# Prompt attention scores as plain float32 products in the two row halves of the array

## The chip, the cores and the metric

One Trainium2 chip, of which the kernel uses one NeuronCore. The core has five engines that run side by side: TensorE (matrix products, with a weight load ahead of each, in the profile PE and PEld), VectorE (DVE), ScalarE (ACT), GpSimd (POOL) and SyncE (SP), which here issues all DMAs. The metric is the device time of one execution in microseconds, less is better; what is given is the median of three runs.

## The reference

The kernel computes one step of a trunk of two layers for 512 prompt tokens and 32 sample tokens (8 sequences of 4 tokens), all in float32, with a model width of 1024. In each layer a normed input is projected, part of the projection goes to a retention group of 4 heads, part to an attention group of 8 heads of 64 columns; both outputs go through one output projection; then comes a feed-forward with a short convolution. Of the attention over the prompt, with which the change deals, the reference says:

```python
for window, dil in DIL_PATTERNS:
    ...
    s = jnp.einsum('brnqhd,brnkhd->brnhqk', qs, kb) * hd ** -0.5
    ...
    s = jnp.where(valid[None, None, :, None], s, -jnp.inf)
    m = jnp.max(s, axis=-1, keepdims=True)
    p = jnp.exp(s - m)
    den = jnp.sum(p, axis=-1, keepdims=True)
    o = jnp.einsum('brnqhk,brnkhd->brnqhd', p / den, vb)
    ...
return combine_by_denominator(outs, lses)
```

The kernel folds the three patterns into one softmax over all earlier keys: a bias that holds the logarithm of how many patterns see a key is added to the scores.

## The kernel before

All activations lie transposed, columns of the model on the 128 partitions and the 544 tokens along the free axis, as two chunks of 272. The big products (projection, output projection, feed-forward) are the main stream: 256 blocks of 128 output columns, and for each block and each 128 rows of weights three products of split parts. [...] ScalarE makes the high part of the weights (`split_w`, line 311), VectorE subtracts to get the low part (`wl` in the profile). The weights come in by DMA six half blocks ahead and are split three half blocks ahead.

Everything else is put between the steps of the main stream while the program is traced. Each job is a generator that yields what its next piece needs. A planner, class `Clock`, estimates from fixed costs when each engine reaches and ends every instruction; class `Stream` lets a piece go (`_ready`, line 180) when its operands should be there by that estimate: a piece of TensorE 0.30 us after them (`MARGIN`, line 145), a piece of another engine 0.25 us before them at the earliest (`SLACK`). The order of instructions on each engine is thus fixed before the kernel runs, and an engine that comes to an instruction whose operands are late waits there, with everything behind it.

Each layer begins with 28 projection blocks. For each pair of heads (`hp`, four pairs) there is a block of values, one of keys and one of queries; VectorE turns keys and queries by the rotary tables (`ra` once and `rb` four times a block, `rotary_out`, line 486), GpSimd adds the two terms into the tiles `ka` and `qa` (lines 494 and 495). The two heads of a pair lie in partitions 0 to 63 and 64 to 127 of the same tile. `att_pair` (line 544) then does a pair: it transposes the values, splits queries and keys, and runs `att_unit` (line 578) for four groups of 128 queries; unit i sees (i + 1) x 128 keys. `pairs` (line 919) runs pairs 0 and 2 in one generator and pairs 1 and 3 in another.

The split of a pair, for each of its two heads: ScalarE copies the head's queries to float32r (`qq`, 64 partitions) and its keys twice (`kk`, into both halves), VectorE subtracts to get the low part of the queries (into the other half of `qq`) and of the keys (`kl`). The scores of a unit are four products in float32r: for each head [q hi; q lo] x [k hi; k hi], over all 128 rows of the array, then for each head q hi x k lo, over its 64 rows; the second adds to the first in PSUM.

After the scores, for each head of a unit: VectorE adds the bias and takes the row maximum (`p<-sec,cst`), ScalarE takes the exponential with its sum, VectorE takes the reciprocal and scales `p`, TensorE transposes `p` (`sec<-cst,p`), ScalarE copies that out (`pt`), and TensorE multiplies by the values (`sec<-pt,vt`, the two heads in the array's column halves).

All tensor instructions go through one helper, so nearly all rows of the profile have line 112; operations are told apart by their tiles (`sec` is a PSUM tile of this side work, `ps` one of the main stream). Plain float32 products and products of the split parts both read as f32 there.

Of the kernel before, what the change touches and what calls it, by code (L numbers as in the profile page):

```python
# [9 lines left out]
F32 = mybir.dt.float32  # L10
F32R = mybir.dt.float32r
AF = mybir.ActivationFunctionType
OP = mybir.AluOpType
PSUM = bass.MemoryType.PSUM

DEPTH, D, SEQ, NB, T = 2, 1024, 512, 8, 4
# [41 lines left out]


class Clock:  # L60
    """Estimates when each engine reaches and ends the instructions that were traced, so that
    independent work is traced where its operands are likely to be there."""

    def __init__(self):
        self.now = dict.fromkeys(SEM, 0.0)
# [26 lines left out]


class Engine:
    """Hands instructions on to an engine of the core and to the clock."""

    def __init__(self, clock, kind, eng):
        self.clock, self.kind, self.eng = clock, kind, eng
# [16 lines left out]
    def charge(self, method, outs, ins, args, kw):  # L115
        c, kind = self.clock, self.kind
        n = free_size(outs[0]) if outs else 0
        if method == "dma_start":
            c.now["sp"] = max(c.now["sp"], c.when("sp", ins)) + 0.06
            c.dma = max(c.dma, c.now["sp"] + 0.8) + n * outs[0].shape[0] * 4 / 3.6e5  # L120
            c.wrote[c.key(outs[0])] = ("sp", c.dma + 1.0)
            return
        if kind == "pe":
            rows = outs[0].shape[0]
            if method == "transpose":
                cost = max(n, 128) * 2 / 2400
            elif (kw["lhsT"]).dtype == F32R:
                cost = max(n / 2400, 0.107)
            else:
                cost = max(n * 4 / 2400, 0.21) / (1 if rows > 64 else 128 // rows)  # L130
            cost += 0.003
        elif kind == "act":
            ptr = sum(free_size(i) == 1 for i in ins[1:])
            cost = 1.3 if method.startswith("preload") else n / 1200 + 0.093 * (1 + ptr)
        elif kind == "dve":
            half = method in ("tensor_scalar", "tensor_copy")
            cost = (n * (0.5 if half else 1) + 66 + (60 if len(ins) > 2 else 0)) / 960
        else:
            cost = 0.1 + n * (2.2 if len(ins) > 1 else 1.0) / 1000
        c.issue(kind, outs, ins, cost)  # L140
# [9 lines left out]


class Stream:
    """Places pieces of independent work between the steps of the main product stream. A generator
    yields what its next piece needs: its kind (the tensor engine, another engine, or a condition),
    its operands and its banks of PSUM."""

    def __init__(self, clock, share):
        self.clock = clock
# [66 lines left out]
def trunk(ctx: ExitStack, tc: tile.TileContext, xin, w_in, w_out, w_up, w_down, kc, vc, s0, sctx_d, params_d,  # L225
          consts_d, rope_d, y_o, kv_o, pret_o, sret_o, conv_o):
    nc = tc.nc
    clock = Clock()
    pe, act, dve, pool, sp = (Engine(clock, k, e) for k, e in (
        ("pe", nc.tensor), ("act", nc.scalar), ("dve", nc.vector), ("pool", nc.gpsimd), ("sp", nc.sync)))  # L230
# [3 lines left out]
    work = ctx.enter_context(tc.tile_pool(name="work", bufs=1))  # L234
# [10 lines left out]
    def blk(shape, dt=F32, s="b"):  # L245
        return work.tile(shape, dt, name=name(s), tag="blk", bufs=NBLK)

    def PE(*aps, banks=0):
        return need("pe", *aps, banks=banks)

    def EW(eng, *aps):
        return need(eng, *aps)
# [36 lines left out]
    def small(shape, s, bufs):  # L289
        return work.tile(shape, F32, name=name(s), tag=s, bufs=bufs)  # L290

# [1 line left out]
    main = []  # L293
    halves = []

# [7 lines left out]
    raw, split = {}, {}  # L303
# [29 lines left out]
        st.until(lambda: s in split)  # L333
        return split[s]

# [1 line left out]
    x = [cpool.tile([128, 2, HC], F32, name=f"x{n}") for n in range(KB)]  # L337
    par = cpool.tile([128, NPAR], F32, name="par")
    taps = cpool.tile([128, NCONV], F32, name="taps")
# [1 line left out]
    eps = cpool.tile([128, 1], F32, name="eps")  # L341
# [7 lines left out]
        st.until(lambda: len(evacs) < 2)  # L349
        return rotate(psum.tile([128, 2, 512], F32, name=name("ps"), tag="main", bufs=2), "main", 2)  # L350

# [1 line left out]
    class Norm:  # L353
        def __init__(self, idx):
            self.idx = idx
# [43 lines left out]
            return self.parts[k]  # L399

        def rsqrt(self, ps, shape):
            """Yields its steps; returns 1 / sqrt(mean + eps), with a Newton step on the table's value."""
            r, v, t = (blk(shape, F32, s) for s in ("rstd", "var", "tmp"))
            yield EW("act", *ps)
            for c, p in enumerate(ps):
                act.activation(r[:, c], p[:, :HC], AF.Ln, bias=eps, scale=1.0 / D)
            act.activation(r, r, AF.Exp, scale=-0.5)
            for c, p in enumerate(ps):
                dve.tensor_scalar(v[:, c], p[:, :HC], -0.5 / D, -0.5 * EPS, op0=OP.mult, op1=OP.add)
            done(len(ps))  # L410
            yield EW("dve", r)
            dve.tensor_mul(t, r, r)
            yield EW("dve", t)
            dve.tensor_mul(t, t, v)
            yield EW("dve", t)
            dve.scalar_tensor_tensor(r, t, 1.5, r, op0=OP.add, op1=OP.mult)
            return r
# [8 lines left out]
            self.rstd = yield from self.rsqrt(ps, [128, 2, HC])  # L426

    class Last(Norm):
        """Takes the last product stream by halves of the tokens."""

        def take(self, n, c, ps):
            if n == 0:
# [42 lines left out]
    def rhs_of(norm):  # L475
        return norm.part

# [1 line left out]
    def two(ap, w):  # L479
        return ap.rearrange("p (c n) -> p c n", c=2)  # L480

# [40 lines left out]
            st.spawn(gen(ps), "evac")  # L522
        return start

# [1 line left out]
    class Layer:  # L526
        pass

# [11 lines left out]
        for t in L.tab[first]:  # L540
            pool.tensor_mul(t, t, norm.rstd)

    # prompt attention of one pair of heads
    def att_pair(L, l, hp):
        q, k, v = L.qa[hp], L.ka[hp], L.va[hp]
        yield PE(v, banks=2)
        ps = sec([128, 4, 128])
        for c in range(4):
            pe.transpose(ps[:, c, :], v[:, c * 128:(c + 1) * 128], ident)
        ps2 = sec([32, 128])  # L550
        pe.transpose(ps2, v[:, SEQ:NT], ident)
        L.va[hp] = None
        yield EW("act", ps)
        vt = blk([128, 4, 128], F32, "vt")
        act.activation(vt, ps, AF.Copy)
        act.activation(L.vs[:, hp * 128:(hp + 1) * 128], ps2, AF.Copy)
        done(2)
        # float32 products as f32r parts: [q hi; q lo] x [k hi; k hi], then q hi x k lo
        qs, ks = [], []
        kl = blk([128, SEQ], F32R, "kl")  # L560
        for s in range(2):
            r, o = slice(64 * s, 64 * s + 64), slice(64 - 64 * s, 128 - 64 * s)
            kk, qq = blk([128, SEQ], F32R, "kk"), blk([128, SEQ], F32R, "qq")
            yield EW("act", q, k)
            act.activation(qq[r], q[r, :SEQ], AF.Copy)
            act.activation(kk[r], k[r, :SEQ], AF.Copy)
            act.activation(kk[o], k[r, :SEQ], AF.Copy)
            yield EW("dve", qq, kk)
            dve.tensor_sub(qq[o], q[r, :SEQ], qq[r].bitcast(F32))
            dve.tensor_sub(kl[r], k[r, :SEQ], kk[r].bitcast(F32))  # L570
            qs.append(qq)
            ks.append(kk)
        del q, k
        L.qa[hp] = L.ka[hp] = None
        for i in range(4):
            yield from att_unit(L, hp, i, qs, ks, kl, vt)

    def att_unit(L, hp, i, qs, ks, kl, vt):
        n = (i + 1) * 128
        ps, pr, ms, pts = [], [], [], []  # L580
        yield PE(*qs, *ks, kl, banks=2)
        for s in range(2):
            r = slice(64 * s, 64 * s + 64)
            t = sec([128, 512])
            pe.matmul(t[:, :n], lhsT=qs[s][:, i * 128:(i + 1) * 128], rhs=ks[s][:, 0:n], start=True, stop=False)
            ps.append(t)
        for s in range(2):
            r = slice(64 * s, 64 * s + 64)
            pe.matmul(ps[s][:, :n], lhsT=qs[s][r, i * 128:(i + 1) * 128], rhs=kl[r, 0:n], start=False, stop=True)
        for s in range(2):  # L590
            yield EW("dve", ps[s])
            p = blk([128, 512], F32, "p")
# [14 lines left out]
        for s in range(2):  # L607
            yield PE(pr[s], banks=1)
            t = sec([128, 4, 128])
# [9 lines left out]
        for j in range(i + 1):  # L619
            for s in range(2):  # L620
                pe.matmul(po[64 * s:64 * s + 64, :], lhsT=vt[:, j, 64 * s:64 * s + 64], rhs=pts[s][:, j, :],
                          start=j == 0, stop=j == i)
# [6 lines left out]
        L.steps += 1  # L629
        return IF(lambda: st.block >= at)  # L630

    # sample attention of four sequences; rows are (sequence, head, token)
    def att_sample(L, l, g):
        rows = [slice(32 * i, 32 * i + 32) for i in range(4)]
        for hp in range(4):
# [100 lines left out]
        L.cath[k] = (h, lo)  # L736
        L.cat[k] = None

    # retention of one head
    def ret_head(L, l, h):  # L740
        q, k, v = L.qr[h], L.kr[h], L.vr[h]
        qd = blk([128, 4, 128], F32, "qd")
# [6 lines left out]
        ps = sec([128, 4, 128])  # L749
# [7 lines left out]
        ps = sec([128, 4, 128])  # L757
# [7 lines left out]
        ps = sec([128, 4, 128])  # L765
# [4 lines left out]
        sm = blk([128, 4, 128], F32, "sm")  # L770
        dve.tensor_mul(sm, ps, C["dmask"][:, None, h * 128:(h + 1) * 128].to_broadcast([128, 4, 128]))
        done()
        # sample parts of this head
        yield PE(k, v, q, banks=1)
        ps = sec([32, 4, 128])
        pe.transpose(ps[:, 0, :], k[:, SEQ:NT], ident)
# [118 lines left out]
                store(sret_o[l, h, :, g * 4:g * 4 + 4, :], s)  # L895
        L.s0 = None

# [1 line left out]
    def mixer(l):  # L899
        L = Layer()  # L900
        norm = norms[l][0]
# [174 lines left out]
        for n in range(KB):  # L1076
            add_block(w_out[l, n, :, 0:4, :], 4, lambda k: L.cath[k], add_ret(n), pre=pre_ret if n == 0 else None)

# [1 line left out]
    def ffn(l):  # L1080
        norm, nxt = norms[l][1], norms[l + 1][0]
        F = Layer()
# [94 lines left out]
        mixer(l)  # L1177
        ffn(l)

# [1 line left out]
    first = norms[0][0]  # L1181
    act.preload_act_table_set("natural_log_exp_and_others")
    dve.memset(ones, 1.0)
    dve.memset(eps, EPS)
    sp.dma_start(par, params_d[:, :NPAR])
    # keeps the tensor engine's clock up until the first operands are there
    warm = sec([128, 512])
    for _ in range(WARM):
        pe.matmul(warm[:, :128], lhsT=ones, rhs=ones, start=True, stop=True)
# [28 lines left out]
                pe.matmul(ps[:, c, :HC], lhsT=w[wi][:, k - k0, :], rhs=r[ri][:, c, :],  # L1218
                          start=k == 0 and j == 0, stop=k == b["nk"] - 1 and j == 2)

    # the first two blocks run side by side while x arrives
    main[0]["pre"]()
    sp.dma_start(cst[0], consts_d[:, :EARLY])
    ps = [main_bank() for _ in range(2)]
# [36 lines left out]
        b["evac"](ps)  # L1261
        st.pump()

    # the last products run by halves of the tokens, so that the first half's norm and output overlap the second
    main[-KB]["pre"]()
    for c in range(2):
        for n, b in enumerate(main[-KB:]):
# [144 lines left out]
```

## Time and profile before

| | |
|---|---|
| Median of three runs (1456.01 to 1456.38 us) | 1456.33 us |
| Span of the profiled execution | 1455.7 us |
| TensorE busy | 1428.8 us, 98% |
| VectorE busy | 975.1 us, 67% |
| ScalarE busy | 598.8 us, 41% |
| GpSimd busy | 183.1 us, 13% |
| Layer 0, attention over the prompt | about 40 to 175 us of the span |
| Layer 1, the same | about 755 to 892 us |

The span is that of one execution with the profiler on; the median is 0.6 us above it. Busy is the time in which at least one instruction of the engine ran. Matrix products overlap: a record of 272 columns lasts some 290 ns, though the next begins some 125 ns after it, so the cost of a product is read from start to start. A plain float32 product shows as two records, a float32r product as one.

### The profile page before, as it was taken

The numbers are of one execution on the slowest core, as the hardware profiler recorded it, in microseconds if no ns is written. First come the engines' busy times: TensorE is split into PE (matmuls) and PEld (weight loads), VectorE is DVE, ScalarE is ACT, GpSimd is POOL, SyncE is SP. The second block draws the span as 40 slices with busy tenths as digits, with TensorE's granted clock in tenths as the row PEclk, the third lists the DMA queues.
The fourth block names the chain that finished last, engine by engine and source line by source line (L and its number), as shares of the span: only waits on it lengthen the run. The fifth ranks groups of instructions, "written<-read, shape, count | busy, mean of one in ns | idle before, by whom it ended". The sixth has DMA issues, their size and how long they took to land.

```text
span 1455.7 us, 29739 instructions
## 1 busy us (share of the span) xinstructions
PE 1428.8 (98%) x11634; PEld 1364.1 (94%) x11634; DVE 975.1 (67%) x1889; ACT 598.8 (41%) x1156; POOL 183.1 (13%) x553
## 2 busy tenths in 40 slices
PE   8998999999999999999999999999999999999997
PEld 8987887999999999999998888889999999999996
DVE  8977645588775565656678776446977746566665
ACT  4456423444443333323434554224544424333334
POOL 4323211000000000000023221110000000000003
PEclk9999999999999999999999999999999999999999
DMA  6232387433223223223322234863332231322231
GB/s 235 97 104 87 105 275 285 153 123 109 88 81 94 87 75 103 95 83 106 107 90 91 95 103 140 319 230 115 124 111 88 70 118 63 102 87 96 86 98 62
DMA packets 98635, 173.92 MB, mean 119 GB/s; under 512 B 11072, under 2 KB 21440, under 8 KB 98496
## 3 DMA queue, kind: packets, MB, share of 16 engines
q1 hardware_dynamic: 98496, 172.03, 35.1%
q8 instruction: 92, 1.51, 0.4%
q14 instruction: 47, 0.39, 0.1%
HBM read 159.77 MB, written 12.21 MB: 118 GB/s over the span
## 4 chain that ended last, share of the span: by engine, by line
PE 89%; DVE 7%; issue 2%; ACT 1%; DMA 1%; SPq 0%; DVEq 0%; ACTq 0%
PE ps L112 78%; PE sec L112 11%; DVE rb L112 2%; DVE wl L112 2%; DVE p L112 1%; DVE qq L112 0%; DMA kt<-kc 0%; DMA x<-xin 0%; DVE ra L112 0%; ACT p L112 0%; SPq L112 0%; DVE kl L112 0%; DVE xl L112 0%; DVE pm L112 0%; DVE sq L112 0%
## 5 line engine op out<-in xcount | busy, mean ns | idle before, releaser
L112 PE MATMUL ps<-xh,wh 128*128 128x272 f32 x2304 | 490.7, 294 | 1.3 <-ACT wh L112 1.1
L112 PE MATMUL ps<-xh,wl 128*128 128x272 f32 x2304 | 478.1, 289 | 1.4 <-DVE wl L112 1.4
L112 PE MATMUL ps<-xl,wh 128*128 128x272 f32 x2304 | 476.8, 288 | 0.0
L112 PEld LDWEIGHTS ps<-xh,wh 128*128 128x128 f32 x2304 | 362.4, 190 | 12.4 <-issue 7.8
L112 PEld LDWEIGHTS ps<-xh,wl 128*128 128x128 f32 x2304 | 362.4, 189 | 1.6 <-DVE wl L112 1.6
L112 PEld LDWEIGHTS ps<-xl,wh 128*128 128x128 f32 x2304 | 362.4, 189 | 0.1
L112 ACT ACTIVATE wh<-raw 128x512 fp32r<-128x512 f32 (+2 forms) x432 | 247.7, 598 | 172.1 <-PE ps L112 155.9
L112 DVE TENSOR_TENSOR wl<-raw,wh 128x512 fp32r<-128x512 f32 (+2 forms) x432 | 296.7, 705 | 18.4 <-ACT wh L112 17.6
L112 DVE SCALAR_TENSOR_TENSOR c<-u,taps,c 128x560 f32<-128x560 f32 x176 | 141.1, 802 | 88.6 <-ACT c L112 85.5
L112 ACT ACTIVATE c<-u,taps 128x560 f32<-128x560 f32 x88 | 75.4, 856 | 226.6 <-DVE u L112 223.2
L112 DVE TENSOR_TENSOR x<-x,ps 128x544 f32<-128x544 f32 (+1 forms) x120 | 81.6, 680 | 119.8 <-PE ps L112 119.3
L112 PE MATMUL ps<-yh,wh 128*128 128x272 f32 x704 | 150.9, 288 | 0.0
L112 PE MATMUL ps<-yh,wl 128*128 128x272 f32 x704 | 150.5, 288 | 0.0
L112 PE MATMUL ps<-yl,wh 128*128 128x272 f32 x704 | 150.4, 288 | 0.0
L112 DVE TENSOR_TENSOR u<-ps,rstd 128x512 f32<-128x512 f32 (+1 forms) x176 | 69.1, 435 | 80.3 <-PE ps L112 80.3
L112 PEld LDWEIGHTS ps<-yl,wh 128*128 128x128 f32 x704 | 112.2, 188 | 0.1
L112 PEld LDWEIGHTS ps<-yh,wh 128*128 128x128 f32 x704 | 112.2, 188 | 0.1
L112 PEld LDWEIGHTS ps<-yh,wl 128*128 128x128 f32 x704 | 112.2, 188 | 0.0
L112 POOL COPY last<-u 128x2 f32<-128x2 f32 (+1 forms) x176 | 28.0, 191 | 665.6 <-DVE u L112 658.8
L112 DVE TENSOR_TENSOR rb<-ps,rope 32x544 f32<-32x544 f32 (+1 forms) x96 | 69.2, 721 | 1.4
L112 ACT ACTIVATE yh<-y 128x544 fp32r<-128x544 f32 x44 | 29.0, 658 | 82.6 <-DVE y L112 82.6
L112 ACT ACTIVATE p<-p,pm 128x128 f32<-128x128 f32 (+3 forms) x64 | 35.5, 556 | 58.6 <-DVE pm L112 57.1
(153 smaller groups left out, 1439.4 us busy)
## 6 DMA issues: line engine op xcount, KB each, us to landing
raw<-w_up SPq DMA_DIRECT2D x176, 256.0 KB, 2.8
raw<-w_in SPq DMA_DIRECT2D x112, 256.0 KB, 3.6
kt<-kc SPq DMA_DIRECT2D x80, 256.0 KB, 4.6
vt<-vc SPq DMA_DIRECT2D x80, 256.0 KB, 4.8
raw<-w_down SPq DMA_DIRECT2D x48, 256.0 KB, 2.7
raw<-w_out SPq DMA_DIRECT2D x32, 256.0 KB, 2.9
raw<-w_down SPq DMA_DIRECT2D x32, 192.0 KB, 2.4
s<-s SPq DMA_DIRECT2D x16, 256.0 KB, 5.5
```

The lines of the kernel that those rows point to most:

```text
L112: return f(*args, **kw)
```

## The change

The splitting of queries and keys is taken out of `att_pair`: per pair of heads six copies on ScalarE and four subtractions on VectorE, and the tiles `kl`, `kk` (two) and `qq` (two). `att_unit` gets the tiles `qa` and `ka` themselves and runs one plain float32 product for each head in place of two of split parts, the first head in rows 0 to 63 of the array and the second in rows 64 to 127, each into its own bank of PSUM. The tiles `qa` and `ka` are held until the fourth unit of their pair is traced. The planner's cost of a plain float32 product, which was divided for few output rows alone, is now also divided by two where the product is over 64 rows. The rest of the diff takes out comments and docstrings (not shown).

```diff
             else:
-                cost = max(n * 4 / 2400, 0.21) / (1 if rows > 64 else 128 // rows)
+                side = min(rows, kw["lhsT"].shape[0])
+                cost = max(n * 4 / 2400, 0.21) / (1 if side > 64 else 128 // side)
             cost += 0.003
...
         act.activation(L.vs[:, hp * 128:(hp + 1) * 128], ps2, AF.Copy)
         done(2)
-        # float32 products as f32r parts: [q hi; q lo] x [k hi; k hi], then q hi x k lo
-        qs, ks = [], []
-        kl = blk([128, SEQ], F32R, "kl")
-        for s in range(2):
-            r, o = slice(64 * s, 64 * s + 64), slice(64 - 64 * s, 128 - 64 * s)
-            kk, qq = blk([128, SEQ], F32R, "kk"), blk([128, SEQ], F32R, "qq")
-            yield EW("act", q, k)
-            act.activation(qq[r], q[r, :SEQ], AF.Copy)
-            act.activation(kk[r], k[r, :SEQ], AF.Copy)
-            act.activation(kk[o], k[r, :SEQ], AF.Copy)
-            yield EW("dve", qq, kk)
-            dve.tensor_sub(qq[o], q[r, :SEQ], qq[r].bitcast(F32))
-            dve.tensor_sub(kl[r], k[r, :SEQ], kk[r].bitcast(F32))
-            qs.append(qq)
-            ks.append(kk)
-        del q, k
         L.qa[hp] = L.ka[hp] = None
         for i in range(4):
-            yield from att_unit(L, hp, i, qs, ks, kl, vt)
+            yield from att_unit(L, hp, i, q, k, vt)

-    def att_unit(L, hp, i, qs, ks, kl, vt):
+    def att_unit(L, hp, i, q, k, vt):
         n = (i + 1) * 128
         ps, pr, ms, pts = [], [], [], []
-        yield PE(*qs, *ks, kl, banks=2)
+        yield PE(q, k, banks=2)
         for s in range(2):
             r = slice(64 * s, 64 * s + 64)
             t = sec([128, 512])
-            pe.matmul(t[:, :n], lhsT=qs[s][:, i * 128:(i + 1) * 128], rhs=ks[s][:, 0:n], start=True, stop=False)
+            pe.matmul(t[:, :n], lhsT=q[r, i * 128:(i + 1) * 128], rhs=k[r, 0:n], start=True, stop=True)
             ps.append(t)
-        for s in range(2):
-            r = slice(64 * s, 64 * s + 64)
-            pe.matmul(ps[s][:, :n], lhsT=qs[s][r, i * 128:(i + 1) * 128], rhs=kl[r, 0:n], start=False, stop=True)
```

## Rows read from the trace of the kernel before

**Rows 1.** The page, first part: engine, busy us (share), instructions.
```profile
PE 1428.8 (98%) x11634; PEld 1364.1 (94%) x11634; DVE 975.1 (67%) x1889; ACT 598.8 (41%) x1156; POOL 183.1 (13%) x553
```
**Rows 2.** Stretches: length, busy us of each engine (instructions), granted clock, DMA share, GB/s.
```profile
100.00:120.00 20.00, 17.15 (x129) 15.09 (x128) 17.59 (x35) 7.57 (x22) 8.39 (x9) 1.00 0.36 121
180.00:280.00 100.00, 100.00 (x953) 83.70 (x953) 50.90 (x136) 33.13 (x70) 13.81 (x30) 1.00 0.72 250
820.00:840.00 20.00, 17.81 (x127) 15.40 (x128) 16.08 (x42) 7.96 (x25) 5.45 (x6) 0.91 0.32 110
```
**Rows 3.** Waits of PE, 40 to 175 us, then 755 to 892: us, times, longest.
```profile
PE sec L112 <- DVE p L112: 4.9, 7, 2.2
...
PE sec L112 <- DVE p L112: 4.4, 5, 2.2
```
**Rows 4.** PE in order of time, first units that waited: start, us, instruction [idle before].
```profile
51.75 0.22 PE L112 MATMUL sec<-kk,qq 128*128 128x128 f32 x1
52.52 0.30 PE L112 MATMUL sec<-kk,qq 128*128 128x128 f32 x1 [0.55 <-DVE qq L112]
...
53.40 0.39 PE L112 MATMUL ps<-xh,wh 128*128 128x272 f32 x1
...
144.45 0.31 PE L112 MATMUL sec<-kk,qq 128*128 128x128 f32 x1
...
146.49 0.33 PE L112 MATMUL sec<-pt,vt 128*64 128x128 f32 x2
```
**Rows 5.** PE in order of time: scores of units that did not wait.
```profile
66.19 0.50 PE L112 MATMUL sec<-kk,qq 128*128 128x256 f32 x2
...
66.94 0.52 PE L112 MATMUL ps<-xh,wh 128*128 128x272 f32 x2
...
67.80 0.34 PE L112 MATMUL sec<-kk,qq 128*128 128x128 f32 x2
...
68.32 0.40 PE L112 MATMUL ps<-xh,wh 128*128 128x272 f32 x1
...
86.28 0.73 PE L112 MATMUL sec<-kk,qq 128*128 128x512 f32 x2
86.94 0.50 PE L112 MATMUL sec<-kl,qq 64*128 64x512 f32 x2
87.38 0.33 PE L112 MATMUL sec<-pt,vt 128*64 128x128 f32 x2
```
**Rows 6.** PE in order of time: plain float32 products in parts of the array.
```profile
85.97 0.39 PE L112 MATMUL sec<-pt,vt 128*64 128x128 f32 x4
...
143.64 1.06 PE L112 MATMUL sec<-qr,kr 128*128 128x128 f32 x8
...
219.82 1.06 PE L112 MATMUL sec<-vs,ptn 32*32 32x512 f32 x8
220.81 0.39 PE L112 MATMUL ps<-xh,wh 128*128 128x272 f32 x1
```
**Rows 7.** DVE in order of time, then PE: ahead of the longest wait.
```profile
100.56 1.66 DVE L112 TENSOR_TENSOR qq<-qa,qq 64x512 fp32r<-64x512 f32 x1
...
113.77 0.33 PE L112 MATMUL sec<-cst,p 128*128 128x128 f32 x1 [2.17 <-DVE p L112]
```
**Rows 8.** Groups of PE over the span: busy us, mean ns; the chain in time: start, us.
```profile
L112 PE MATMUL ps<-xl,wh 128*128 128x272 f32 x2304 | 476.8, 288 | 0.0
...
L112 PE MATMUL sec<-kl,qq 64*128 64x512 f32 x16 | 4.0, 495 | 0.0
...
339.02 392.41 PE ps L112 x3126
```
**Rows 9.** ACT in order of time: the first copy of pair 0.
```profile
43.59 0.63 ACT L112 ACTIVATE qq<-qa 64x512 fp32r<-64x512 f32 x1 [4.05 <-POOL qa L112]
```
**Rows 10.** Groups of DVE by form, 40 to 175 us: busy us, mean ns, idle before.
```profile
L112 DVE TENSOR_TENSOR qq<-qa,qq 64x512 fp32r<-64x512 f32 x8 | 7.4, 930 | 0.2
...
L112 DVE TENSOR_TENSOR kl<-ka,kk 64x512 fp32r<-64x512 f32 x8 | 5.5, 691 | 0.3
```

## The prediction

> **What bounds the kernel now.** I began with the busy times. TensorE is busy 98% of the span, VectorE 67%, ScalarE 41% [rows 1]: a faster ScalarE or VectorE gains only where TensorE waits for it. So I looked next, stretch by stretch, for where TensorE is not full. From 180 to 280 us it is busy 100.00 of 100 us with VectorE at half, but in the attention over the prompt it misses up to 2.85 us of 20 [rows 2]. The waits of TensorE in the two attention stretches name the cause: `p`, the softmax rows that it is to transpose, 4.9 us in 7 waits in layer 0 and 4.4 in 5 in layer 1 [rows 3]. The order of time adds first units that stand between two of their own score products until `qq`, a split part of the queries, is there [rows 4], and shows what VectorE did ahead of the longest wait, 2.17 us for `p`: the split of a later pair is part of it [rows 7].
>
> [...]
>
> The change can thus gain in four places: waits for split parts, waits for `p` behind the split on VectorE, the clock, and the scores themselves on TensorE.
>
> **Waits for split parts.** The first unit of a pair, 128 keys, takes 0.52 us from the first score to the next work where nothing is late (67.80 to 68.32) [rows 5]. The first pair's took 1.65 us (51.75 to 53.40), the fourth pair's 2.04 (144.45 to 146.49) [rows 4]. So 1.13 and 1.52 us were waiting; layer 1 repeats both, with 0.88 and 1.51. Sum 5.0 us, which goes with the tiles. What is late next is `qa` itself. GpSimd makes it, and nothing but the values' transposes and their copy now lies between it and the first unit. ScalarE stood 4.05 us for `qa` of pair 0 [rows 9] while TensorE went on. The planner sent ScalarE there too early, and will send TensorE 0.55 us (0.30 plus 0.25) later by its own count. The new wait of pair 0 is thus between 0 and 4 us a layer, with the main stream queued behind it on TensorE. I take 1.2, nearer to nothing: ScalarE had been idle before it, so most of its 4.05 us need not be the planner's error. Pairs 2 and 3 start only when another pair has ended, long after their queries. Net 5.0 - 2.4 = 2.6 us, bounds -3.0 to 5.0.
>
> **Waits for `p`.** Those rows give 4.9 + 4.4 = 9.3 us idle in 12 waits [rows 3]. An idle time is counted from the record's end, and a main product's record lasts 288 ns where the next begins 392.41 / 3126 = 126 ns after it [rows 8], so each wait hides 0.16 us more: 9.3 + 12 x 0.16 = 11.2 us. The split holds VectorE 7.4 + 5.5 = 12.9 us a layer [rows 10], and some of it stands right ahead of the waits: in the 14 us before that of 2.17 a `qq` of 1.66 us [rows 7], another and two `kl` at the usual 0.69 [rows 10], 3.7 us together. Were the order to stay, nearly all would go. It won't: units that need no split come earlier, into stretches where rotary sums and weights fill VectorE anyway, and the planner goes on to price VectorE too low. I take half, 5.6 us, bounds 0 to 11.2; below nothing is a rival.
>
> ScalarE loses 24 copies a layer of 0.63 us [rows 9], 15 us, all beside TensorE's work: nothing by itself, being idle over half the time [rows 1].
>
> **The clock.** 0.91 over 20 us is 1.8 us of array time, twice [rows 2]: 3.6 us. Shorter waits should end some of it. I take one of the two, 1.8 us, bounds -1.8 (one more) to 3.6.
>
> **The scores on TensorE.** Before, where nothing was late, a unit takes 0.52 us for 128 keys, 0.75 for 256 (66.19 to 66.94) and 1.10 for 512 (86.28 to 87.38) [rows 5], halfway for 384, 0.92. No row shows plain float32 in row halves. The nearest is plain float32 in row- and column-limited tiles: eight records of 512 columns, four products side by side, from 219.82 to 220.81, 0.99 us with the way out [rows 6]. A plain product of 128 columns over the full array takes 0.81 / 4 = 0.20 us (143.64 to 144.45) [rows 4, 6], so 512 alone are some 0.85, and 0.14 is for the changes of shape. If the two heads run side by side, a unit takes 0.99, 0.78, 0.56 and 0.35 us for 512 to 128 keys (0.213 less each time). Into the row shape from a main product I add 0.09 us, about two thirds of that 0.14; the old first product needed none. The savings are 0.52 - 0.35 - 0.09 = 0.08, then 0.19, 0.14 and 0.11; times eight units each, 4.2 us. Six units of the middle sizes follow a main product instead of the values' column halves (four of 256 keys, two of 384); theirs I count as nothing: 4.2 - 4 x 0.19 - 2 x 0.14 = 3.1. [...] I take 3.0, as the nearer row is plain float32 too.
>
> **Edits with no cost.** Two tiles held longer and five fewer made leave more of the 51 buffers free. The sample attention, which follows the pairs, starts earlier with its loads, which pass the weights' on SP; DMA is at 0.72 where they run now [rows 2], under 0.37 before, and weights are fetched six halves ahead. If that cover were gone, a late half block would stop the main stream for its 3 us. The planner's new divisor touches only these products.
>
> **The sum.** 2.6 + 5.6 + 1.8 + 3.0 = 13.0 us. The profiled execution goes from 1455.7 to 1442.7 us of span; the median lies 0.6 above, so 1443.3 us.
>
> **Rivals.** One: the waits stay and change their name. VectorE's rotary sums and weights alone fill it in the stretches before the waits, `p` stays as late, `qa` takes the place of `qq`. Then only the scores gain: 1456.3 - 3.0 = 1453.3. For it: the planner's errors stay. Against: 12.9 us a layer leave VectorE.
>
> Two, on the other side: the heads do not run side by side, so the change does not do what it says. Then each unit pays its streaming twice, 0.213 + 0.427 + 0.640 + 0.853 = 2.13 us a pair, 17.1 for eight: 1460.4. It decides the sign once three quarters of the overlap are lost (13.0 of 17.1). For it: no row shows that form. Against: the old `kl` products ran in row halves side by side (16 records of 495 ns cover 4.0 us, so each pair lies over itself) [rows 8], and plain float32 ran in column halves, two products of 128 in 0.31 us with the change of shape (85.97 to 86.28) [rows 5, 6], where two in turn take 0.40.
>
> Three: the overlap is only half. A plain product is two records, and if the second record of head one had to come before the first of head two, a unit would need three rounds for two: half of 17.1, 8.5 us, so 1451.8. Against it: with that order, the four tiles of [rows 6] would need five rounds, over 2 us instead of 0.99. [...]
>
> Four: units brought forward crowd VectorE between 40 and 62 us, and the waits for `p` grow by half instead: 1456.3 + 5.6 - 3.0 + 1.8 (one more stretch at half clock) = 1460.7. Against: VectorE has less to do in all.
>
> Five: nearly all waits go, a gain near 20: 1436.
>
> **How the numbers follow.** Chances: forecast 0.58 (1437 to 1450), waits renamed 0.17 (1450 to 1456), no overlap 0.08, half overlap 0.05, crowding 0.06, all waits gone 0.06. The range 1437 to 1455 leaves out no overlap, crowding, most of the last and a little of the second. A measurement can tell about 0.2%, 2.9 us, from no change. Faster by more: 0.58 + 0.05 + 0.06 + half of 0.17 = 0.77; same 0.11, from the other half and edges; slower 0.12.
>
> **What would show it.** Right: no `qq`, `kk` or `kl`; the two heads' scores starting within a few ns and 512 keys taking 1.0 us; waits for `p` near 5 us in all; at most one dip of the clock in layer 1. Wrong: a unit of 512 keys near 1.85 us (no overlap), waits on GpSimd's `qa` over 2 us a layer, or waits for `p` still above 9 us.

## The result, and the profile after

The changed kernel takes 1444.86 us (median of four, 1444.67 to 1444.93) against 1456.36 (four, 1456.01 to 1456.99) for the kernel before on the same chip: ratio 0.992 [0.9906, 0.9934], 11.5 us less. The forecast was 1443.3 in a range of 1437 to 1455, and faster. The span fell from 1455.7 to 1443.0 us, by 12.7.

The page's first part of the kernel after, which answers [rows 1]:

```profile
PE 1423.1 (99%) x11634; PEld 1356.0 (94%) x11634; DVE 949.2 (66%) x1857; ACT 571.6 (40%) x1108; POOL 178.9 (12%) x553
```

TensorE runs as many instructions as before. VectorE has 32 fewer and 25.9 us less to do, ScalarE 48 fewer and 27.2 less. Next the waits of TensorE in the two attention stretches, 40 to 175 us and then 740 to 885 (us in all, times, longest), which answer [rows 3]:

```profile
PE sec L112 <- DVE p L112: 2.5, 2, 1.8
PE sec L112 <- POOL qa L112: 0.5, 1, 0.5
PE sec L112 <- ACT pt L112: 0.3, 1, 0.3
...
PE sec L112 <- DVE p L112: 2.5, 2, 1.7
PE sec L112 <- ACT pt L112: 0.3, 1, 0.3
```

Waits for `qq` are gone, those for `p` went from 9.3 us in 12 to 5.0 in 4, and the new wait for `qa` is 0.5 us, once. Four stretches of 20 us (length, busy us of each engine with instructions, granted clock, DMA share, GB/s), for [rows 2]:

```profile
100.00:120.00 20.00, 20.00 (x168) 17.47 (x167) 15.95 (x34) 8.94 (x22) 5.18 (x8) 1.00 0.41 137
...
800.00:820.00 20.00, 20.00 (x169) 17.23 (x168) 13.70 (x39) 10.12 (x31) 2.14 (x3) 1.00 0.16 54
840.00:860.00 20.00, 18.21 (x146) 15.88 (x147) 14.31 (x27) 9.64 (x23) 7.44 (x13) 1.00 0.25 79
860.00:880.00 20.00, 20.00 (x225) 17.01 (x222) 10.65 (x38) 3.89 (x10) 1.88 (x2) 1.00 0.70 248
```

Where TensorE lost 2.85 us of 20 before, 100 to 120, it is now full. The one bad stretch of layer 1, 840 to 860, holds the wait of 1.7 us for `p`, and the granted clock is 1.00 there too: both dips to half clock in layer 1 are gone. Before, one is that of 820 to 840 in [rows 2], the other this (kernel before, columns as above):

```profile
860.00:880.00 20.00, 19.08 (x144) 16.91 (x143) 14.29 (x53) 9.13 (x31) 2.55 (x9) 0.91 0.39 134
```

In stretches of 2 us both stand at 0.50, from 830 to 832 and from 864 to 866. TensorE in order of time, start, us, instruction [idle before], at the scores, for [rows 4, 5]:

```profile
43.04 0.49 PE L112 MATMUL sec<-ka,qa 64*128 64x128 f32 x4 [0.53 <-POOL qa L112]
...
58.09 0.49 PE L112 MATMUL sec<-ka,qa 64*128 64x128 f32 x4
58.51 0.39 PE L112 MATMUL ps<-xh,wh 128*128 128x272 f32 x1
...
65.13 0.70 PE L112 MATMUL sec<-ka,qa 64*128 64x256 f32 x4
65.76 0.39 PE L112 MATMUL ps<-xh,wh 128*128 128x272 f32 x1
...
87.77 1.13 PE L112 MATMUL sec<-ka,qa 64*128 64x512 f32 x4
88.83 0.39 PE L112 MATMUL ps<-xh,wh 128*128 128x272 f32 x1
```

From the first score to the next work a unit now takes 0.42 us for 128 keys, 0.63 for 256, 1.06 for 512, where it took 0.52, 0.75 and 1.10 [rows 5]. Each unit is four records, two a head. Last, for [rows 8], the groups by form over the span (records, busy us, mean ns, idle before):

```profile
L112 PE MATMUL sec<-ka,qa 64*128 64x512 f32 x32 | 9.0, 641 | 0.0
...
L112 PE MATMUL sec<-ka,qa 64*128 64x128 f32 x32 | 3.9, 323 | 0.6 <-POOL qa L112 0.5
```

The two longest pieces of the chain that ended last (start, us, products):

```profile
333.21 391.43 PE ps L112 x3126
...
1041.32 376.76 PE ps L112 x3000
```

The 32 records of 512 keys last 641 ns each, 20.5 us if laid end to end; they cover 9.0. So the records of two heads lie over one another. The chain's pieces are the feed-forward of the two layers: 0.98 us shorter in layer 0 than in [rows 8], and in layer 1 no shorter, of which more below.

### The profile page after: what moved, and what is told of

It reads as the page before. It is cut to its first block, busy times and chain, and to the rows that moved or that the text cites. A ratio compares the mean times of both kernels' runs of the same rounds, so it can differ in the third digit from the quotient of the medians.

```text
span 1443.0 us, 29646 instructions
## 1 busy us (share of the span) xinstructions
PE 1423.1 (99%) x11634; PEld 1356.0 (94%) x11634; DVE 949.2 (66%) x1857; ACT 571.6 (40%) x1108; POOL 178.9 (12%) x553
## 4 chain that ended last, share of the span: by engine, by line
PE 94%; DVE 3%; issue 1%; DMA 0%; ACT 0%; SPq 0%; DVEq 0%; POOL 0%; ACTq 0%
PE ps L112 82%; PE sec L112 12%; DVE wl L112 1%; DVE rb L112 1%; DMA x<-xin 0%; DVE p L112 0%; SPq L112 0%; DVE xl L112 0%; DVE ra L112 0%; DVE sq L112 0%; ACT xh L112 0%; DVE va L112 0%; POOL qa L112 0%; DVEq L1381 0%; DVE tmp L112 0%
## 5 line engine op out<-in xcount | busy, mean ns | idle before, releaser
L112 PE MATMUL ps<-ch,wh 128*128 128x272 f32 x256 | 53.4, 290 | 0.0
```

The lines of the kernel that those rows point to most:

```text
L112: return f(*args, **kw)
```

## The experiments

Two readings of the result stood against each other. Theory: VectorE has less to do, so `p` comes in time; whatever is left of the waits comes from the planner's too low prices for VectorE. Rival: the gain comes from scores that no longer stand for split parts and from the new order that the planner writes, and a wait taken away there turns up again at the next `p`.

The kernel before was timed beside every run. Its medians are 1456.36 us for the result and the first four runs, then 1456.83 and 1456.97 on other chips. The ratios below are against the kernel before on the same chip; differences between two runs on different chips are uncertain by some 0.6 us.

**The split kept, its results unread.** The split's ten instructions a pair are put back into the changed kernel. The planner holds a unit back until the split parts are there, as before (`asked` is `qs`, `ks` and `kl`), but the scores read `qa` and `ka`.

```diff
+        qs, ks = [], []
+        kl = blk([128, SEQ], F32R, "kl")
...
-        yield PE(q, k, banks=2)
+        yield PE(*asked, banks=2)
```

> The changed kernel with the splitting of queries and keys put back on ScalarE and VectorE, in its old place; nothing reads its results, and the planner holds the scores back until they are there by its count, so the order is that of before. The scores are the plain products. Theory (VectorE's work ahead of the waits for p is a gain of its own, apart from the wait for the split parts): only the waits for split parts go, 5.3 us, and 0.6 us of the scores; the waits for p stay at some 11 us: 1450.5 us, 1447 to 1453. Rival (VectorE is simply late, and a wait that is taken away turns up at the next p): 1455.7 us, with waits for p of some 16 us. Rival (only the waits for split parts ever mattered): 1445, as the changed kernel.

Measured: 1460.40 us (1460.04 to 1461.62), ratio 1.0029 [1.0018, 1.0041]: slower than before. Waits of TensorE, layer 0 and layer 1:

```profile
PE sec L112 <- DVE p L112: 7.7, 7, 3.0
...
PE sec L112 <- DVE p L112: 7.5, 7, 3.0
```

No score waits for anything, and the waits for `p` rose from 9.3 to 15.2 us; the time is 4.7 us above what even the rival expected. The order is close to that of before but not the same, as the planner prices the new scores otherwise. The first pair shows where the waits went. Before, unit 0 lost 1.13 us to `qq` [rows 4], and the next transpose of `p` stood 1.03 more, as TensorE's order of time has it (kernel before):

```profile
60.73 0.30 PE L112 MATMUL sec<-cst,p 128*128 128x128 f32 x1 [1.03 <-DVE p L112]
```

With the split unread (this kernel, the same view), unit 0 runs at once in 0.42 us, and the same transpose stands 2.08:

```profile
51.86 0.49 PE L112 MATMUL sec<-ka,qa 64*128 64x128 f32 x4
52.28 0.52 PE L112 MATMUL ps<-xh,wh 128*128 128x272 f32 x2
...
60.69 0.45 PE L112 MATMUL sec<-cst,p 128*128 128x128 f32 x1 [2.08 <-DVE p L112]
```

The transpose begins at 60.7 us in both. 1.13 + 1.03 = 2.16 became 2.08: the wait only changed its name, as the rival says. Behind it the clock fell (this kernel in stretches of 2 us, columns as above):

```profile
60.00:62.00 2.00, 1.31 (x6) 1.34 (x7) 1.88 (x7) 1.98 (x7) 0.00 (x0) 0.63 0.00 0
62.00:64.00 2.00, 2.00 (x11) 2.00 (x10) 1.82 (x4) 1.95 (x5) 0.00 (x0) 0.52 0.91 273
```

Beside one in the first 20 us, at 10.3 us in the kernel before and in the changed one, this kernel has three such dips in its profiled execution: in the chain that ended last the main products from 61.14, 120.47 and 836.79 us stand 0.227 us apart in place of 0.125. The kernel before has two. What the products themselves gain is too little to show beside that.

**The order kept, the work gone.** The same kernel, but the planner is only charged for the split: it books price and due time, and no instruction is issued. The order on TensorE, VectorE and ScalarE is that of the experiment above, instruction by instruction.

```diff
+            for d, src in ((qq, q), (kk, k), (kk, k)):
+                act.charge("activation", [d], [src], (), {})
+            yield EW("dve", qq, kk)
+            for d, src, hi in ((qq, q, qq), (kl, k, kk)):
+                dve.charge("tensor_sub", [d], [src, hi], (), {})
```

> The changed kernel without the splitting, but the planner still charges its engines for it, so the order of the instructions is that of before and the work is gone. Theory (the waits for p stand behind the split's 3.7 us on VectorE, and the changed kernel gives part of the gain back by bringing units forward): waits for p fall from 11 to 2 or 3 us, no dip of the clock in layer 1: 1456.4 - 5.3 - 8.5 - 2.8 - 0.6 = 1439 us. Rival (the new order is what gains, the work on VectorE not): waits for p stay near 11 us, 1450 us.

Measured: 1446.16 us (1445.95 to 1446.17), 0.993 [0.9914, 0.9947]. Waits, layer 0 and 1:

```profile
PE sec L112 <- DVE p L112: 2.1, 5, 0.7
...
PE sec L112 <- DVE p L112: 2.1, 5, 0.7
```

14.2 us went with the work alone, in an order that was written for a kernel that has the split. No dip of the clock is left: the mean granted clock is 0.996 in each of the four executions, against 0.992 to 0.993 in those of the split kept. Against this the new order of the changed kernel (1444.86) brings only 1.3 us, and the next run comes to 1444.50 without it; so nothing of the gain can be put down to the new order. In this order the gain is the work, as the theory has it, though 4.2 us of waits remain and the time is not the 1439 that it expected.

**Which half of the split.** The same order again, first with the copies issued and the subtractions only charged, then the reverse.

```diff
             act.activation(kk[o], k[r, :SEQ], AF.Copy)
             yield EW("dve", qq, kk)
-            dve.tensor_sub(qq[o], q[r, :SEQ], qq[r].bitcast(F32))
+            dve.charge("tensor_sub", [qq[o]], [q[r, :SEQ], qq[r]], (), {})
...
```

> As the run with the splitting kept (1460.4 us), but only ScalarE's six copies a pair are done; VectorE's four subtractions are gone, and the planner still charges for all, so the order stays that of before. Theory (VectorE's work is what makes p late): as the run in which all splitting was gone in the order of before, 1446 us, waits of TensorE in the two attention stretches of some 4 us. Rival (ScalarE's copies delay the exponentials and with them p): 1453 us or more.

Measured: 1444.50 us (1444.33 to 1444.96), 0.9915 [0.99, 0.993], with 4.4 us of waits for `p`, none over 0.7. ScalarE's 48 copies cost nothing that can be seen: the time is even 1.7 us below that without them, for which no cause was shown.

In the reverse the subtractions are issued on the queries and keys themselves, since the high parts are not made; nothing reads their results.

```diff
-            act.activation(qq[r], q[r, :SEQ], AF.Copy)
+            act.charge("activation", [qq[r]], [q[r, :SEQ]], (), {})
...
-            dve.tensor_sub(qq[o], q[r, :SEQ], qq[r].bitcast(F32))
+            nc.vector.tensor_sub(qq[o], q[r, :SEQ], k[r, :SEQ])
+            dve.charge("tensor_sub", [qq[o]], [q[r, :SEQ], qq[r]], (), {})
...
```

> The run with VectorE's subtractions alone, once more: in the earlier one the planner, seeing other operands, had put the pieces in another order, so it did not compare with the runs that it was made for. Now the planner is charged exactly as with all splitting kept, so every engine's order is that of those runs; VectorE's four subtractions a pair are done, ScalarE's six copies are not. Theory (VectorE's work is what costs): near 1460 us, waits of TensorE of some 15 us in the two attention stretches. Rival (it takes both halves of the split, the copies holding up the subtractions): 1448 us, as in the earlier run.

Measured: 1461.63 us (1461.11 to 1462.01), 1.0031 [1.002, 1.0043], and the waits are those of the whole split:

```profile
PE sec L112 <- DVE p L112: 7.6, 7, 3.0
...
PE sec L112 <- DVE p L112: 7.4, 7, 2.9
```

Thirty-two subtractions on an engine that is busy 67% cost 15.5 us more than their absence in the same order. An earlier kernel issues the same subtractions on the same operands, but there the planner too was given these operands, so that it wrote a third order:

> The other half: VectorE's four subtractions a pair are done (on the queries and keys themselves, the results are not read), ScalarE's six copies are gone, the planner charges for all. Theory (VectorE's work is what makes p late): as with all splitting kept, 1458 to 1461 us, waits of TensorE of some 15 us. Rival (ScalarE's copies): 1446 us.

Measured: 1448.28 us (1447.79 to 1449.93), 0.9944 [0.9928, 0.9961]. Page, first part, and the waits of layer 0 and 1:

```profile
PE 1425.2 (99%) x11634; PEld 1356.0 (94%) x11634; DVE 967.5 (67%) x1889; ACT 570.1 (39%) x1108; POOL 179.0 (12%) x553
```

```profile
PE sec L112 <- DVE p L112: 3.5, 3, 2.1
...
PE sec L112 <- DVE p L112: 3.2, 3, 1.8
```

VectorE has its 1889 instructions here as in the kernel before, all 32 subtractions among them, yet the waits for `p` are 6.7 us and the mean granted clock of the profiled execution is 0.996, near the changed kernel's 0.997. The theory's 1458 to 1461 missed. In this order the subtractions cost some 2 to 3 us against the kernels without them (1446.16 and 1444.86). Why this order bears them was not tried.

**The subtractions in the new order.** The changed kernel with four unread subtractions a pair behind its first unit, of which the planner is not told; the order is otherwise that of the changed kernel.

```diff
             yield from att_unit(L, hp, i, q, k, vt)
+            if i == 0:
+                for s in range(2):
+                    r, o = slice(64 * s, 64 * s + 64), slice(64 - 64 * s, 128 - 64 * s)
+                    qq = blk([128, SEQ], F32R, "qq")
+                    nc.vector.tensor_sub(qq[o], q[r, :SEQ], k[r, :SEQ])
+                    nc.vector.tensor_sub(qq[r], k[r, :SEQ], q[r, :SEQ])
```

> The changed kernel with four subtractions a pair on VectorE (64 partitions x 512, not read by anything) put behind the first unit of the pair, of which the planner is not told, so that the order stays that of the changed kernel. Theory (in the new order too, VectorE's spare time in these stretches is less than the 22 us of the split): 1455 to 1460 us. Rival (the new order has room for it; the old order was the trouble): 1445 to 1448 us.

Measured: 1461.51 us (1461.11 to 1462.35), 1.0033 [1.0021, 1.0045], 16.6 us above the changed kernel. Page, first part, and the waits of layer 0 and 1:

```profile
PE 1428.6 (98%) x11634; PEld 1357.0 (93%) x11634; DVE 972.9 (67%) x1889; ACT 571.4 (39%) x1108; POOL 181.9 (12%) x553
```

```profile
PE sec L112 <- DVE p L112: 5.9, 6, 1.8
PE sec L112 <- DVE pm L112: 1.9, 2, 1.3
...
PE sec L112 <- DVE p L112: 5.5, 5, 1.8
PE sec L112 <- DVE pm L112: 2.0, 2, 1.2
```

23.7 us more of VectorE make 15.3 us of waits for `p` and `pm`, where there were 5.0. With 0.16 us hidden in each wait, as the forecast counted, that is 10.3 + 0.16 x 11 = 12.1; two dips of the clock (main products 0.20 and 0.23 us apart from 159.36 and 781.53 us) cost 1.7 each, an estimate that takes them to be as long as the two of the kernel before, 3.41 us at half clock; 15.5 of the 16.6 are accounted for. In these two orders the subtractions cost about the same, so the changed kernel's new order is not what gains. But the third order above carries them for 2 to 3 us: what they cost depends on where they stand on VectorE, and not on their 22 us alone.

**The scores twice.** Each unit's two products are issued a second time into the same tiles, for the price of the scores by themselves.

```diff
+        for s in range(2):
+            r = slice(64 * s, 64 * s + 64)
+            pe.matmul(ps[s][:, :n], lhsT=q[r, i * 128:(i + 1) * 128], rhs=k[r, 0:n], start=True, stop=True)
```

> The changed kernel with each pair of score products done twice into the same banks (the second overwrites the first). It prices the streaming of the scores without the way in and out. Theory (side by side, 0.213 us for each 128 keys of a unit, all on TensorE's path): 8 x 2.13 = 17.1 us more, 1462 us, a little less where it fills a wait. Rival (the heads run in turn, or half so): 34 or 26 us more, 1471 to 1479 us.

Measured: 1468.76 us (1467.35 to 1469.29), 1.008 [1.0065, 1.0095], 23.9 us above the changed kernel. TensorE in order of time:

```profile
86.79 1.99 PE L112 MATMUL sec<-ka,qa 64*128 64x512 f32 x8
88.71 0.52 PE L112 MATMUL ps<-xh,wh 128*128 128x272 f32 x2
...
97.50 0.72 PE L112 MATMUL sec<-ka,qa 64*128 64x128 f32 x8
98.15 0.51 PE L112 MATMUL ps<-xh,wh 128*128 128x272 f32 x2
```

512 keys take 1.92 us instead of 1.06: the second pair of products adds 0.86 us for two heads, twice 430 ns. One after another they would have added 1.72. For 384, 256 and 128 keys 0.65, 0.43 and 0.22 come on top, 2.16 us a pair, 17.3 in all. Of the other 6.6, some 5.5 are waits for `p`, which grew from 5.0 us in 4 to 9.8 in 14, less those for `pt`, which are gone. So the heads run side by side without loss once the array is in that shape.

**What is left of the waits.** On VectorE the planner charges 66 cycles an instruction beside one per column (half of one for scalings and copies). The rotary products of 544 columns take 0.72 us in the trace, which at the planner's 960 cycles a us is 691, so 147 beside the columns. The subtractions that make the weights' low part last 0.418, 0.551 and 0.684 us for 256, 384 and 512 columns in the trace of before (medians), so 145 beside the columns by the same count. The scalings of `p` last 0.287 us for 128 columns and 0.487 for 512, so 211 beside a half for each column. The changed kernel with these prices:

```diff
-            cost = (n * (0.5 if half else 1) + 66 + (60 if len(ins) > 2 else 0)) / 960
+            cost = (n * (0.5 if half else 1) + (200 if half else 150)) / 960
+            if method == "tensor_tensor_reduce":
+                cost += 0.08
```

> The changed kernel with the planner's prices of VectorE raised to what the trace shows: a fixed part of 0.156 us (0.208 for scalings) in place of 0.069, and 0.08 us more for the row maximum. No instruction changes, only their order. Theory (the waits that are left, 5 us for p and 1 us for pt and qa, come from prices that are too low): they fall to 1 or 2 us, 1440.5 us. Rival (VectorE is full in these stretches whatever the order): 1445 us.

Measured: 1439.19 us (1438.78 to 1440.18), 0.9884 [0.9869, 0.9899], faster than the changed kernel by 5.7. Waits from 30 to 175 us, then of layer 1:

```profile
PE ps L112 <- DVE va L112: 2.4, 1, 2.4
PE sec L112 <- DVE p L112: 0.3, 1, 0.3
...
PE sec L112 <- DVE p L112: 0.4, 1, 0.4
```

Waits for `p` are nearly gone, and with them the waits for `qa` and `pt`. One new wait of 2.4 us stands where the changed kernel has 0.3: the main stream waits for the values `va`, two of which take VectorE 3.08 us (this kernel, VectorE in order of time):

```profile
28.14 3.08 DVE L112 TENSOR_TENSOR va<-ev,rstd 128x512 f32<-128x512 f32 x2
```

The changed kernel, in the same view, makes them in 1.96:

```profile
27.67 1.96 DVE L112 TENSOR_TENSOR va<-ev,rstd 128x512 f32<-128x512 f32 x2
```

GpSimd multiplies the rotary tables at that time in both; why the two products take 1.1 us more in one was not settled. A blunter way to the same end is the planner's margin, the time by which an operand must be due before TensorE is sent to it:

```diff
-MARGIN = 0.3
+MARGIN = 1.0
```

> The changed kernel with the planner's margin for TensorE's pieces at 1.0 us in place of 0.3. Theory (the waits left are errors of the planner's clock of up to 2 us): each is shortened by 0.7 us, 6 of them: 1441 us. Rival (the pieces come later, and VectorE's own next pieces with them, so the waits only move): 1445 us.

Measured: 1442.00 us (1440.52 to 1442.38), 0.99 [0.9886, 0.9915], 0.4 us of waits for `p` and the same 2.4 for `va`. Two more tried to mend prices further. A GpSimd sum of two tensors, priced at 3.2 ns a column in place of 2.2, as the rows of its sums into `ka` and `qa` have it (1.64 to 1.80 us for 512):

> The changed kernel with VectorE's prices as in the run at 1439.2 us, and GpSimd's price of a sum raised by 45% to what the trace shows (1.75 us for 512). Only the order changes. Theory (what is left are the planner's errors): the 2.6 us wait for va and the waits of 0.5 us for p shrink, 1437 us. Rival (the waits left are contention between GpSimd and VectorE): 1439 to 1440 us.

gave 1442.46 us (1441.44 to 1445.16), 0.9907 [0.9891, 0.9924], and the same with a margin of 0.5 us

> The same with the margin for TensorE's pieces at 0.5 us in place of 0.3. Theory: the last waits for p go, 1436.5 us. Rival (nothing left to gain from the order): as without it, within 1 us.

gave 1439.55 (1438.66 to 1440.62), 0.9881 [0.9867, 0.9896]: no wait for `p` at all, a wait of 2.7 for `va`, and no gain over the VectorE prices alone.

**Would better prices have done it without the change?** The kernel before with VectorE's fixed part at 110 cycles (160 for the scalings); the full prices were not tried there.

> The kernel before, with the planner's prices of VectorE raised part of the way (fixed part 0.115 us, 0.167 for scalings, in place of 0.069, and 0.08 more for the row maximum). Only the order changes. Theory (the waits come from VectorE's work and from prices that are too low for it, so that the split in the old kernel costs less when it is priced right): half of the 17 us of waits go, 1448 us. Rival (VectorE is full, no order helps the kernel that splits): 1455 to 1457 us.

Measured: 1455.05 us (1453.74 to 1456.03), 0.9988 [0.9979, 0.9998]. Layer 0's waits, which layer 1 repeats but for 0.4 in place of 0.6:

```profile
PE sec L112 <- DVE pm L112: 3.8, 1, 3.8
PE sec L112 <- DVE p L112: 0.9, 1, 0.9
PE sec L112 <- DVE qq L112: 0.6, 1, 0.6
```

Fewer waits, but one of 3.8 us a layer, and the mean granted clock is 0.991 to 0.992 in its ten executions, where the kernel before has 0.993 to 0.996 on that chip. At these prices the gain is 1.8 us (the kernel before took 1456.83 on that chip). Whether the kernel before with the full prices, or in an order like the third one above, would come near the changed kernel was not tried and stays open.

## Why the prediction was right

The range, the sign and the main mechanism held; the size was 13.0 us against 11.5. The runs divide the change in three steps: plain scores with the split's work and its due times kept, +4.0 us; the work taken away in that order, -14.2; the planner told of it, -1.3, no more than two kernels of one order differ by (1446.16 and 1444.50). By the forecast's own terms:

- **Waits for split parts** (2.6, from 5.0 less 2.4). The 5.0 are gone and the new waits are 0.53 + 0.16 = 0.7 in layer 0, nothing to speak of in layer 1: 4.3 by the rows. GpSimd's `qa` stood nearer to nothing than the 1.2 a layer taken, so the size was off by 1.7. But the term was not worth that by itself, and here the forecast's reasoning failed: "5.0 us, which goes with the tiles" took the waits to end with their operands. With the split kept and unread they went over to `p`, to 0.08 us in the first pair. This is the rival "waits renamed", true of the tiles and false of the change, as the change also takes away VectorE's work.
- **Waits for `p`** (5.6 of 11.2). Measured 5.0 + 4 x 0.16 = 5.6 left, so 5.6 gone, as forecast; new waits for `pt` take back 0.9. Half was a choice between bounds, and it hit. Of the two reasons given for the rest, the planner's low prices are the one that the runs show: with prices set to the rows, 0.7 us idle remain of the 5.0, with the same work. Whether crowding by units that come earlier has a part in it is not told apart, as the new prices also move the units.
- **The two together.** The forecast split into two terms what is one: 32 subtractions. Put back alone, they cost 15.5 us in the order planned for the split and 16.6 in that of the changed kernel, waits and clock together; 2.6 + 5.6 + 1.8 = 10.0 was forecast for this. In a third order they cost 2 to 3; so what this term is worth hangs on the order that the planner writes, for which the forecast had no more than its choice of a half.
- **ScalarE's copies** (nothing). 1444.50 with them, 1446.16 without, in the same order: no cost, as forecast.
- **The clock** (1.8, one of two dips). Both are gone. Layer 1's attention gained 7.8 us, of which 4.2 are waits and 0.4 scores, which leaves 3.2; [rows 2] made it 3.6, and two stretches of 3.4 us at half clock in the trace of before make 3.4. The first begins at 829.5 us, behind the wait of 2.19 us for `p`; the second, at 863.6, has no idle time over 0.81 us in the 20 us ahead of it. The term was mis-sized by one dip.
- **The scores** (3.0). The heads run side by side, the first record of the second head 7 ns after that of the first, the second records of both 533 and 540 ns after. But the unit is 0.07 us longer than forecast at each size (0.42, 0.63, 1.06 for 0.35, 0.56, 0.99). The step that failed is the price of the changes of shape, 0.14 us, taken from the 32-row, 32-column tiles of [rows 6]: the first of the two rounds of 512 columns takes 533 ns where a round of the second copy in the doubled scores takes 430, so 0.10 on the first round, and the way out takes 0.10 too. The way in from a main product is 0.09, as forecast. (The 0.85 for 512 keys held, as the second copy takes 0.86; the 0.20 that it was said to follow from gives 0.81.) Counted over all 32 units, from the first score to the next work where nothing waits, the gain is 0.6 to 0.9 us.

The terms as measured, 4.3 + 5.6 - 0.9 + 3.2 + 0.9 = 13.1, are near the 13.0 us gained in the two attention stretches; the clock's 3.2 is what was left over there, so part of the fit is built in. That 13.1 also meets the forecast's 13.0 is luck: split parts and clock came out 1.7 and 1.4 above their terms, `p` with the new waits for `pt` 0.9 below, the scores 2.1 below. By place, counted at the main products: 0.6 us ahead of the attention, 5.2 in layer 0's, 7.8 in layer 1's, and 0.9 in layer 0's feed-forward are gained, and 1.9 in layer 1's are given back, 12.6 in all. The two in the feed-forward are the pace of the main stream. In layer 1 it is 376.76 us for 3000 products, 125.6 ns each, where before (the chain in time) it was 125.0:

```profile
1055.76 375.03 PE ps L112 x3000
```

In these long stretches all kernels run the same kind of products, and the pace lies between 125.0 and 125.6 ns in eight of them. That is up to 2 us a stretch; its cause was not tried and stays open. It was in no term of the forecast. A last 1.2 us: the times of the later kernels lie 1.8 us above their spans, and the forecast added 0.6. In the executions of the kernel before on record the time lies some 2 us above the span too, so the profiled one, of 1455.7 us, presumably took longer than the median.

Of the rivals: no overlap and half overlap are refuted (1.06 us for 512 keys, where no overlap would take 1.85 and half overlap, at three rounds, some 1.4; 0.86 added by a doubled unit). Half overlap needs head one's second record ahead of head two's first; in the trace head one's two start at 0 and 533 ns, head two's at 7 and 540. Crowding on VectorE did not come: waits for `p` fell. That nearly all waits go was not what the change did, but what it allowed: with VectorE priced by its rows the kernel takes 1439.2.

## What to carry to other kernels

When a wait goes because its operand is no longer needed, ask whether the engine that was late has less to do: if not, the wait turns up at its next result. Work on an engine that is busy two thirds of the span cost two thirds of its duration here (16.6 us for 23.7), where it stands in front of what the busiest engine needs next, and in another order some tenth of it (2 to 3 us for 18.3); copies on another engine right beside it cost nothing (1444.50 us with the 48, 1446.16 without). So before work is taken out, ask whether another order would carry it. A planner that orders work by estimated prices should have them set to the profile's rows: here that was worth half as much again as the change (5.7 us on top of 11.5).

## What the runs showed of the hardware

- Plain float32 products of 64 rows, one in each half of the array, run at once: a round of 512 columns for both heads takes 430 ns, and each product is two rounds. For 128 columns a doubled unit adds 0.22 us for both heads, and one product over the full array takes as much (eight records in 1.06 us, the last 0.275 long, so 0.112 a record [rows 6]). The changes of shape cost more than those of the 32-row, 32-column tiles: 0.10 us on the first round and 0.10 on the way out, where 0.14 was forecast for both.
- The clock's answer to a wait varied, and its length did not tell what came. With the split kept, and with its subtractions alone in the same order, the longest wait is 3.0 us a layer, and both layers have a stretch at lower clock (main products 0.227 us apart from 120.47 and 836.79 us, and from 120.04 and 836.72). With part of the prices in the kernel before the longest is 3.8, and the mean clock 0.991 to 0.992. With the subtractions in the new order the longest is 1.8, with one such stretch a layer. Of the waits between 0.8 and 2.2 some had a stretch at lower clock at their end or behind them (2.19 at 828.86 us in the kernel before, with half clock from 829.46 to 832.87; 0.81, the longest idle time ahead of its second dip, at 863.59; 2.08 with the split kept, with 0.63 and then 0.52) and some had not (2.17 in [rows 7], with 1.00 in [rows 2]; 0.81 at 145.57 us in the same kernel, with 1.00 from 144 to 152; 1.75 and 1.73 in the changed kernel, with 1.00 in both stretches of 20 us). The waits of 2.7 for `va` go with a mean clock of 0.997 with GpSimd's price and of 0.995 with the margin of 0.5 beside it.
- Executions of one kernel differ in this too. With GpSimd's price three executions of 1441.44 to 1442.82 us show a mean clock of 0.996 to 0.997, and the fourth, of 1445.16 us, shows 0.993. The profile is of one execution, so its dips are not those of the median.
